# One layer of a hybrid encoder in fast matrix products: the first block's x turned token tile by token tile, its squares split anew, and four other places reordered

## The chip, the cores and the metric

The kernel runs on one core of a Trainium2 chip. The metric is the device time of one execution in microseconds, taken over several runs; lower is better. A core has five engines that run side by side, each working through its own instructions in order: TensorE (PE in the profile; PEld is its loading of weights), VectorE (DVE), ScalarE (ACT), GpSimd (POOL) and SyncE (SP), which here only issues DMAs. Matrix products leave TensorE in eight PSUM banks; everything else works in SBUF, and DMAs move data between SBUF and DRAM.

## The reference

For one sequence of 1024 tokens of width 2048, in float32:

```python
h = rms_norm(x, norm_w)
proj = h @ w_in                       # 2048 -> 6656 columns
rq, rk, rv, rg, aq, ak, av, ag = jnp.split(proj, splits, axis=-1)
y_ret = retention_branch(rq, rk, rv, decay_fwd, decay_bwd, gn_w, gn_b) * silu(rg)
y_att = window_attention_branch(aq, ak, av, sink) * silu(ag)
x = x + concat([y_ret, y_att]) @ w_out
return rms_norm(x, final_norm_w)
```

The retention branch has 8 heads of 128. It rotates q and k, and runs a forward and a backward scan in chunks of 128 tokens, each head with its own decay for each direction: the decay is exp(log_sigmoid(d) x distance). The two scans are added and normalised per head. The attention branch has 8 query heads on 2 key and value heads, sees 128 tokens to either side, and has a learned sink logit per head.

## The kernel before

**Arithmetic.** Each float32 operand is split in two fp32r parts: ACT casts the high part (line 87), DVE subtracts it from the source for the low part (line 84, `low`). One product of 128x128 by 128x512 is then three matmuls (lines 98 to 100, `mm3`). The projections use a scheme of fast products: a block of 512 columns by one half of the 2048 features is computed with seven products, numbered `PRODUCTS = (1, 2, 6, 5, 7, 3, 4)`, instead of eight, at the price of sums and differences of quarters of both operands.

**The order of the work.** There are 26 units of work, (feature half, block of columns), in four phases: `EARLY` blocks on half 0; `EARLY` and `LATE` on half 1; `LATE` and `GATES` on half 0; `GATES` on half 1. After them come four units of the output projection (`OUT`), each of seven products. `advance()` is called after every six matmuls of the projections; it raises `clock[0]` and lets every job that is under way take one step. So jobs (turning the second half of x, keeping and reloading combined operands, attention, retention, gating) are generators, whose `yield` hands back to the matmuls until the next such tick, and `idle(n)` waits n ticks.

The order of instructions on PE, SP and POOL is that in which the code is written (`manual_schedule`, line 113). ACT and DVE are ordered by the framework's planner instead, from its own timing; only within `all_manual` (line 415, closed at line 293, at the end of the first block) do all five keep the written order.

**The weights' operands.** `prepare()` (line 265) takes the next weight operand, made by `operand` or `wide`: one cast `wH` on ACT and one subtraction `wL` on DVE. Two are kept (`AHEAD = 2`), and one is made while the one before it is used.

**The first block** (`first_block`, line 269) is computed without the fast scheme, in 8 steps of 4 ticks, while x is still being prepared. Tiles 0 to 7 of x are 128 tokens each; only features 0 to 1023 are needed here. Before the first matmul, `squares(t)` (line 342) sums the squares of a tile's two halves, the first on ACT and the second on DVE (both on ACT for tiles 4 and 5); a small addition on DVE and a power on POOL make 1/rms; `scale_x(t)` (line 356) multiplies the tile on DVE. `turn_x` (line 367) transposes one block of 128 features for the four tiles of one token half, and ACT evicts it, scaled by the norm's weight, which was itself turned from `vec` (lines 414 to 422). `rest_of_x` (line 846) does the other feature blocks and the second token half between ticks: turns of block k at ticks 1 to 4, squares and scalings of tiles 4 to 7 behind them, the turns of the second token half from tick 12, the sums for the fast scheme, and `put(i)`, which makes the combined operand of product i, at the ticks written in line 871. `second_part` (line 390) and `keep` (line 370) are started behind the puts.

**Retention** (`retention`, line 601) begins by loading the decays and computing their logarithms by a series of 9 terms, in small operations on 128x16 values (lines 616 to 636), then waits until the reloads (`to_load`) are through and runs its 8 heads, one after the other. **Gating** (`gating`, line 1035) loads pairs of a mixed tile and its gate, one pair every two ticks (line 1072); ACT computes SiLU and DVE multiplies (`mix_in`), six pairs behind the loads.

**The output projection** (lines 1178 to 1218) evicts each finished bank by adding it to a tile that holds the residual (`out_evict`). In the last two units `summed` (line 1123) squares the sum on ACT, and either weights it with the final norm's weight and adds up the partial sums of squares (`part`), or, if it completes a row, calls `finish` (line 1142): 1/rms on DVE and POOL, two multiplications on DVE, one on ACT, and the row's store.

Of the kernel before, what the change touches and what calls it, by code (L numbers as in the profile page):

```python
# [53 lines left out]
AHEAD = 2  # L54


@with_exitstack
def hybrid_layer_kernel(
# [210 lines left out]
    def first_block(b, of):  # L269
# [23 lines left out]
        all_manual.close()  # L293
# [48 lines left out]
    def squares(t):  # L342
        ss = st.tile([P, 2], F32, name="ss", bufs=4)
        c = [slice(i * PART, (i + 1) * PART) for i in range(2)]
        junk = [wp.tile([P, S], BF16, name="junk", tag="ct", bufs=8) for i in range(2)]
        for i in range(2):
            if i == 0 or t in (4, 5):
                nc.scalar.activation(out=junk[i], in_=xt[t][:, c[i]], func=AF.Square, accum_out=ss[:, i:i + 1])
            else:
                nc.vector.tensor_tensor_reduce(out=junk[i], in0=xt[t][:, c[i]], in1=xt[t][:, c[i]], scale=1.0, scalar=0.0,  # L350
                                               op0=ALU.mult, op1=ALU.add, accum_out=ss[:, i:i + 1])
        rs = rms[:, t:t + 1]
        nc.vector.tensor_scalar(out=rs, in0=ss[:, 0:1], scalar1=ss[:, 1:2], scalar2=D * NORM_EPS, op0=ALU.add, op1=ALU.add)
        nc.gpsimd.tensor_tensor(out=rs, in0=rs, in1=neg_half[:, 0:1], op=ALU.pow)
# [35 lines left out]
    def second_part():  # L390
# [19 lines left out]
        for sums, _ in parts[1]:  # L410
# [5 lines left out]
    all_manual.enter_context(tc.manual_schedule(engines={mybir.EngineType.PE, mybir.EngineType.SP, mybir.EngineType.Pool,  # L416
                                                         mybir.EngineType.Activation, mybir.EngineType.DVE}))
    for t in range(NT):
        load_x(t)
        if t == 0:  # L420
            for r0, n, src in ((0, KT, norm_w), (KT, RH, gn_w), (KT + RH, RH, gn_b)):
                nc.sync.dma_start(out=vec[r0:r0 + n, :], in_=src[0].rearrange("(k p) -> k p", p=P))
# [178 lines left out]
    def retention():  # L601
        with right("ret") as ret:
# [12 lines left out]
            nc.sync.dma_start(out=db, in_=dist_b)  # L615
            nc.vector.tensor_scalar(out=au, in0=dec, scalar1=-1.0, scalar2=None, op0=ALU.mult)
# [7 lines left out]
            for n in (17, 15, 13, 11, 9, 7, 5, 3, 1):  # L624
                nc.vector.tensor_tensor(out=lg, in0=lg, in1=aq, op=ALU.mult)
# [3 lines left out]
            nc.vector.scalar_tensor_tensor(out=lg, in0=lg, scalar=-2.0, in1=dec, op0=ALU.mult, op1=ALU.add)  # L629

# [203 lines left out]
    def advance():  # L834
        clock[0] += 1
        tick()
# [9 lines left out]
    def rest_of_x():  # L846
# [32 lines left out]
    squares(0)  # L879
    for t in range(4):  # L880
        if t < 3:
            squares(t + 1)
        scale_x(t)
        if t == 1:
            pv = ax()
            nc.tensor.transpose(pv[:, 0:KT + 2 * RH], vec, ident[0:KT + 2 * RH, 0:KT + 2 * RH])
            nc.scalar.copy(out=vec_t, in_=pv[:, 0:KT + 2 * RH])
            nc.vector.tensor_scalar(out=nw, in0=nw, scalar1=D ** 0.5, scalar2=None, op0=ALU.mult)
    for s, i in enumerate((1, 2)):
        hold(i, 0)  # L890
        quarters[s + 1, 0] = comb[i][:, 0], comb[i][:, 1]
# [384 lines left out]
```

## Time and profile before

| | us |
|---|---|
| median of 3 runs | 1558.56 |
| lowest, highest | 1552.38, 1559.41 |
| the profiled execution | 1555.15 |
| its span in the profile | 1552.6 |

The page of the profile gives, for each engine, its busy time and share of the span, then the chain of work that ended last, then the groups of like instructions. TensorE's busy time is nearly the whole span, so the question at each place is why it is not busy: the lines of the timeline give the start and the length of an instruction, and in brackets the idle time of its engine just before it and what ended that. The granted clock (`PEclk`) tells when TensorE ran at less than full speed. The ends of matmuls in the records are modelled; their starts are the better measure.

### The profile page before, as it was taken

The page shows a single profiled execution, that of the slowest core. Times are in us where ns is not written, and L with a number is a line of the kernel's source. Part 1 is how long each engine was busy: PE and PEld are TensorE (multiplying, and loading weights), DVE is VectorE, ACT ScalarE, POOL GpSimd, SP SyncE. Part 2 cuts the span into 40 slices and gives each one's busy share as a digit, 9 for nine tenths or more (in the row PEclk, how much of TensorE's full clock was granted, in tenths as well). Part 3 has the DMA queues.
Part 4 walks back from the last instruction along what each step waited for, and adds up shares of the span by engine and source line. Part 5 has one row for each costly group of instructions (what it writes and reads, how often), then busy time and mean ns, then how long its engine had stood idle before and what let it go on. Part 6 is the DMA issues. An engine that isn't in the chain of part 4 may idle for free.

```text
span 1552.6 us, 20710 instructions
## 1 busy us (share of the span) xinstructions
PE 1514.6 (98%) x7377; PEld 1273.9 (82%) x7377; DVE 1086.5 (70%) x2037; ACT 690.9 (44%) x1162; POOL 159.5 (10%) x166
## 2 busy tenths in 40 slices
PE   5999999999999999999999999999999999999996
PEld 4788888788888888878888888888878888888885
DVE  5765585456857585757977797779755966775866
ACT  6643353224535363534344434543444553532425
POOL 1000001111110000001212100001211102020001
PEclk9999999999999999999999999999999999999999
DMA  7277645899764325677777566479698689395746
GB/s 284 84 258 249 225 170 160 234 239 230 185 203 136 122 83 177 228 277 203 150 190 196 162 196 204 155 268 311 164 283 204 141 242 201 83 215 169 212 161 244
DMA packets 160326, 306.60 MB, mean 197 GB/s; under 512 B 15040, under 2 KB 80992, under 8 KB 151776
## 3 DMA queue, kind: packets, MB, share of 16 engines
q1 hardware_dynamic: 140640, 269.63, 51.2%
q0 software_dynamic: 19584, 35.66, 15.2%
q8 instruction: 58, 0.95, 0.3%
q14 instruction: 44, 0.36, 0.1%
HBM read 190.68 MB, written 122.95 MB: 202 GB/s over the span
## 4 chain that ended last, share of the span: by engine, by line
PE 88%; DVE 4%; DMA 4%; ACT 2%; issue 1%; SPq 1%; POOL 0%; POOLq 0%; DVEq 0%; ACTq 0%
PE pj L100 23%; PE pj L98 23%; PE pj L99 23%; PE ax L99 4%; PE ax L100 4%; PE ax L98 4%; PE ax L727 2%; PE ax L462 1%; DMA g<-pr 1%; DVE wL L84 1%; PE ax L540 1%; PE ax L364 1%; DMA yt<-pr 1%; PE ax L774 1%; PE ax L694 1%
## 5 line engine op out<-in xcount | busy, mean ns | idle before, releaser
L98 PE MATMUL pj<-c,wH 128*128 128x512 f32 x1448 | 582.2, 402 | 1.4 <-ACT wH L87 1.4
L100 PE MATMUL pj<-c,wL 128*128 128x512 f32 x1448 | 569.4, 393 | 5.3 <-DVE wL L84 5.3
L99 PE MATMUL pj<-c,wH 128*128 128x512 f32 x1448 | 567.7, 392 | 0.0
L84 DVE TENSOR_TENSOR wL<-a,wH 128x1024 fp32r<-128x1024 f32 x184 | 225.0, 1223 | 173.8 <-ACT wH L87 172.6
L100 PEld LDWEIGHTS pj<-c,wL 128*128 128x128 f32 x1448 | 273.5, 189 | 67.0 <-DVE wL L84 8.5
L98 PEld LDWEIGHTS pj<-c,wH 128*128 128x128 f32 x1448 | 274.0, 189 | 51.3 <-ACT wH L87 1.8
L99 PEld LDWEIGHTS pj<-c,wH 128*128 128x128 f32 x1448 | 274.1, 189 | 49.5
L87 ACT CAST wH<-a 128x1024 fp32r<-128x1024 f32 x184 | 193.4, 1051 | 264.8 <-PE pj L99 117.4
L253 ACT COPY ct<-pj 128x512 f32<-128x512 f32 x200 | 115.9, 584 | 195.3 <-PE pj L100 194.5
L243 POOL DMA_DIRECT2D pr<-ct x104 | 92.2, 961 | 844.3 <-DVE ct L91 733.7
L91 DVE TENSOR_TENSOR ct<-pj,ct 128x512 f32<-128x512 f32 x170 | 114.4, 689 | 80.5 <-PE pj L100 76.5
L99 PE MATMUL ax<-wL,c 128*128 128x512 f32 x224 | 87.4, 390 | 1.8 <-DVE wL L84 1.8
L99 PE MATMUL pj<-wL,c 128*128 128x512 f32 x224 | 87.5, 391 | 0.1
L98 PE MATMUL ax<-wH,c 128*128 128x512 f32 x224 | 87.3, 390 | 0.2 <-DVE r L91 0.2
L100 PE MATMUL ax<-wH,c 128*128 128x512 f32 x224 | 87.3, 390 | 0.0
L100 PE MATMUL pj<-wH,c 128*128 128x512 f32 x224 | 87.3, 390 | 0.0
L98 PE MATMUL pj<-wH,c 128*128 128x512 f32 x224 | 87.3, 390 | 0.0
L87 ACT CAST sH<-st 128x128 fp32r<-128x128 f32 x112 | 31.1, 298 | 51.8 <-DVE st L741 37.7
L84 DVE TENSOR_TENSOR wL<-s,wH 128x1024 fp32r<-128x1024 f32 x31 | 37.7, 1216 | 19.7 <-ACT wH L87 19.7
L99 PEld LDWEIGHTS ax<-wL,c 128*128 128x128 f32 x224 | 42.1, 188 | 10.8 <-DVE wL L84 2.2
L99 PEld LDWEIGHTS pj<-wL,c 128*128 128x128 f32 x224 | 42.1, 188 | 9.5 <-DVE wL L84 0.9
L98 PEld LDWEIGHTS ax<-wH,c 128*128 128x128 f32 x224 | 42.1, 188 | 9.2 <-issue 0.5
(194 smaller groups left out, 2015.4 us busy)
## 6 DMA issues: line engine op xcount, KB each, us to landing
a<-in_w_in_dram SPq DMA_DIRECT2D x104, 512.0 KB, 4.6
kept<-c SPq DMA_DIRECT2D x28, 1024.0 KB, 7.0
c<-kept SPq DMA_DIRECT2D x28, 1024.0 KB, 9.2
pr<-ct SPq DMA_DIRECT2D x104, 256.0 KB, 5.2
pr<-ct POOLq DMA_DIRECT2D x104, 256.0 KB, 6.2
rx<-pr SPq DMA_DIRECT2D x148, 64.0 KB, 4.4
a<-in_w_out_dram SPq DMA_DIRECT2D x18, 512.0 KB, 5.2
xt<-in_x_dram SPq DMA_DIRECT2D x16, 512.0 KB, 8.7
```

What stands on the lines that cost most here:

```text
L84: nc.vector.tensor_tensor(out=dst, in0=src, in1=high.bitcast(F32), op=ALU.subtract)
L87: nc.scalar.copy(out=dst_h, in_=src)
L91: nc.vector.tensor_tensor(out=dst, in0=a, in1=b, op=ALU.add)
L98: nc.tensor.matmul(po, aH, bH, start=first, stop=False, **kw)
L99: nc.tensor.matmul(po, aH, bL, start=False, stop=False, **kw)
L100: nc.tensor.matmul(po, aL, bH, start=False, stop=last, **kw)
L243: nc.gpsimd.dma_start(out=dst, in_=t, accum_op=ALU.add)
L253: nc.scalar.copy(out=t, in_=bank)
L364: nc.tensor.transpose(pt[:, blk(i)], part, ident)
L462: nc.tensor.transpose(pt[:, blk(t)], src[:, blk(b * 4 + t)], ident)
L540: nc.tensor.transpose(pt[:, blk(j)], s[:, blk(j)], ident)
L727: nc.tensor.matmul(p, k_tok[:, c], vd[:, c, d], start=True, stop=True)
```

## The change

The change touches five places.

*First block.* The three loads of `vec` are issued from ACT's queue, ahead of all x loads, instead of from SP's behind the first tile. The transposes of the first token half run token tile by token tile, into four banks (`pts`), each tile's four right behind its scaling, instead of all four tiles for one feature block at a time. Behind tile 1's transposes stand 6, and behind tile 2's 10, transposes of the unit matrix into a bank that nothing reads. `squares` takes one half of a tile at a time, and which engine; of the eight halves of tiles 4 to 7, ACT squares three instead of six, DVE five instead of two, and three of DVE's now stand between the turns of the first four ticks. The second token half is turned from tick 11 instead of 12, and the puts of products 6, 5, 7 and 4 stand at ticks 22, 26, 32 and 37 instead of 23, 25, 33 and 36. The region in which all engines keep the written order ends at tick 33 instead of at the end of the block.

*Decays.* Four ticks pass between the loads of the decays and the first operation on them, and the series is cut in pieces, with a tick ahead of the terms 17, 11 and 5 and one ahead of the exponentials.

*Gating.* A pair is loaded every three ticks instead of two.

*Last rows.* From product 4 of the last unit on, all engines keep the written order. Weightings are put off by three, the finishing of rows by five steps (a step is the three matmuls of one `mm3`). The addition for a row's 1/rms moves from DVE to POOL.

*Last operand.* The weight operand for the second half of the last product is prepared ahead of the last eviction of the product before it.

```diff
+ORDERED = {getattr(mybir.EngineType, n) for n in ("PE", "SP", "Pool", "Activation", "DVE")}
...
-        all_manual.close()
...
-    def squares(t):
...
-            if i == 0 or t in (4, 5):
...
+    def squares(t, i, act):
...
+        if act:
+            nc.scalar.activation(out=junk, in_=c, func=AF.Square, accum_out=ss[:, i:i + 1])
+        else:
+            nc.vector.tensor_tensor_reduce(out=junk, in0=c, in1=c, scale=1.0, scalar=0.0,
+                                           op0=ALU.mult, op1=ALU.add, accum_out=ss[:, i:i + 1])
+        if i == 1:
...
+    for r0, n, of in ((0, KT, norm_w), (KT, RH, gn_w), (KT + RH, RH, gn_b)):
+        nc.scalar.dma_start(out=vec[r0:r0 + n, :], in_=of[0].rearrange("(k p) -> k p", p=P))
     for t in range(NT):
         load_x(t)
-        if t == 0:
-            for r0, n, src in ((0, KT, norm_w), (KT, RH, gn_w), (KT + RH, RH, gn_b)):
-                nc.sync.dma_start(out=vec[r0:r0 + n, :], in_=src[0].rearrange("(k p) -> k p", p=P))
...
             nc.sync.dma_start(out=db, in_=dist_b)
+            yield from idle(4)
...
             for n in (17, 15, 13, 11, 9, 7, 5, 3, 1):
+                if n % 6 == 5:
+                    yield
...
             nc.vector.scalar_tensor_tensor(out=lg, in0=lg, scalar=-2.0, in1=dec, op0=ALU.mult, op1=ALU.add)
+            yield
...
     def advance():
         clock[0] += 1
+        if clock[0] == 33:
+            all_manual.close()
         tick()
...
             turn_and_split(1, k, 0, comb[2])
-        squares(4)
+            if k != 2:
+                squares(*{0: (4, 0), 1: (4, 1), 3: (5, 0)}[k], False)
+        for t in (6, 7):
+            yield
+            if t == 6:
+                squares(5, 1, True)
+            squares(t, 0, True)
+            squares(t, 1, False)
+            scale_x(t - 2)
         yield
-        for t in range(4, NT):
-            if t + 1 < NT:
-                squares(t + 1)
-            scale_x(t)
-            yield
-        yield from idle(12 - clock[0])
+        scale_x(6)
+        scale_x(7)
+        yield from idle(11 - clock[0])
...
-            yield from idle({6: 23, 5: 25, 7: 33, 4: 36}[i] - clock[0])
+            yield from idle({6: 22, 5: 26, 7: 32, 4: 37}[i] - clock[0])
...
+    pts = [ax() for k in range(M)]
+    idling = pj()
...
+    for t in range(5):
+        if t < 4:
+            squares(t, 0, True)
+            squares(t, 1, False)
+        if t > 0:
+            scale_x(t - 1)
+            if t == 4:
+                prepare()
+            for k in range(M):
+                nc.tensor.transpose(pts[k][:, blk(t - 1)], xt[t - 1][:, blk(k)], ident)
+            for _ in range({2: 6, 3: 10}.get(t, 0)):
+                nc.tensor.transpose(idling[:, 0:P], ident, ident)
     for k in range(M):
-        turn_and_split(0, k, 0, comb[1])
+        nc.scalar.activation(out=src0[:, 0, k, half(0)], in_=pts[k], func=AF.Copy, scale=nw[:, k:k + 1])
+        split(comb[1][:, 0, k], comb[1][:, 1, k], src0[:, 0, k, half(0)])
...
-                        yield from idle(2)
+                        yield from idle(3)
...
+    def after(steps, what, *args):
+        later.append((at_now[0] + steps, what, args))
+
+    def due(every=False):
+        while later and (every or later[0][0] <= at_now[0]):
+            _, what, args = later.popleft()
+            what(*args)
...
+        if whole:
+            rs = op.tile([P, 1], F32, name="rs", bufs=4)
+            nc.gpsimd.tensor_scalar(out=rs, in0=ssq[:, tt, 3:4], scalar1=part[tt], scalar2=1.0 / D, op0=ALU.add, op1=ALU.mult)
+            nc.gpsimd.tensor_tensor(out=rs, in0=rs, in1=neg_half[:, 0:1], op=ALU.pow)
+            after(5, finish, rs, r, rt[u, 3 - n, m, t], tt, g)
+        elif u == 3:
+            after(3, weighted, r, tt, g, True)
+        else:
+            weighted(r, tt, g, False)
+            stores.append((True, res[tt][:, half(g)], r))
...
+            if (u, i) == (3, 4):
+                wo_.enter_context(tc.manual_schedule(engines=ORDERED))
...
                 if k == M - 1:
+                    if (u, i, t) == (3, 5, M - 1):
+                        prepare()
                     out_evict(u, i, t, bank[t], held)
+                at_now[0] += 1
+                due()
...
+    due(True)
     wo_.close()
```

More of the change, by code (lines that the diff above doesn't have):

```diff
@@ L340, in load_x @@
             nc.sync.dma_start(out=xt[t][:, c], in_=x[blk(t), c])
-    def squares(t):
[L343 to L346, printed above, removed]
-            if i == 0 or t in (4, 5):
[L348 to L354, printed above, removed]
+    sums_of = {}
+    def squares(t, i, act):
+        if t not in sums_of:
+            sums_of[t] = st.tile([P, 2], F32, name="ss", bufs=4)
+        ss, c = sums_of[t], xt[t][:, i * PART:(i + 1) * PART]
+        junk = wp.tile([P, S], BF16, name="junk", tag="ct", bufs=8)
+        if act:
[4 more added lines that the diff above has]
+        if i == 1:
+            rs = rms[:, t:t + 1]
+            nc.vector.tensor_scalar(out=rs, in0=ss[:, 0:1], scalar1=ss[:, 1:2], scalar2=D * NORM_EPS, op0=ALU.add, op1=ALU.add)
+            nc.gpsimd.tensor_tensor(out=rs, in0=rs, in1=neg_half[:, 0:1], op=ALU.pow)
     def scale_x(t):
@@ L877, in rest_of_x @@
         start(keep(0))
[L879 to L891, printed above, removed]
-    prepare()
+    pv = pj()
+    nc.tensor.transpose(pv[:, 0:KT + 2 * RH], vec, ident[0:KT + 2 * RH, 0:KT + 2 * RH])
+    nc.scalar.copy(out=vec_t, in_=pv[:, 0:KT + 2 * RH])
+    nc.vector.tensor_scalar(out=nw, in0=nw, scalar1=D ** 0.5, scalar2=None, op0=ALU.mult)
+    pts = [ax() for k in range(M)]
+    idling = pj()
+    for i, t in enumerate((1, 2)):
+        hold(t, 0)
+        quarters[i + 1, 0] = comb[t][:, 0], comb[t][:, 1]
+    for t in range(5):
[10 more added lines that the diff above has]
+                nc.tensor.transpose(idling[:, 0:P], ident, ident)
     for k in range(M):
-        turn_and_split(0, k, 0, comb[1])
+        nc.scalar.activation(out=src0[:, 0, k, half(0)], in_=pts[k], func=AF.Copy, scale=nw[:, k:k + 1])
+        split(comb[1][:, 0, k], comb[1][:, 1, k], src0[:, 0, k, half(0)])
     start(rest_of_x())
@@ L1121, in prefill @@
             nc.sync.dma_start(out=e, in_=res[4 * (m - 1) + t][:, half(2 * OUT[u][1] + n - 1)])
+    at_now, later = [0], deque()
+    def after(steps, what, *args):
[4 more added lines that the diff above has]
+            what(*args)
     def summed(u, n, m, t):
         r, tt, g = rt[u, n, m, t], 4 * (m - 1) + t, 2 * OUT[u][1] + n - 1
-        op, fw, ssq = (pools[n] for n in ("op", "fw", "ssq"))
+        op, ssq = pools["op"], pools["ssq"]
         whole = u == 3 and (n, m) in ((2, 1), (1, 2))
@@ L1136, in summed, with finish @@
             nc.vector.tensor_scalar(out=part[tt], in0=part[tt], scalar1=D * NORM_EPS, scalar2=None, op0=ALU.add)
-        if u == 2:
-            stores.append((True, res[tt][:, half(g)], r))
-        if whole:
-            finish(r, rt[u, 3 - n, m, t], tt, g)
-    def finish(r, r1, tt, g):
-        op, fw, ssq = (pools[n] for n in ("op", "fw", "ssq"))
-        rs = op.tile([P, 1], F32, name="rs", bufs=4)
-        nc.vector.tensor_scalar(out=rs, in0=ssq[:, tt, 3:4], scalar1=part[tt], scalar2=1.0 / D, op0=ALU.add, op1=ALU.mult)
-        nc.gpsimd.tensor_tensor(out=rs, in0=rs, in1=neg_half[:, 0:1], op=ALU.pow)
+    def finish(rs, r, r1, tt, g):
         g1 = 4 * OUT[3][1] + 1 - g
-        row = rows_a[tt]
+        fw, row = pools["fw"], rows_a[tt]
         nc.vector.scalar_tensor_tensor(out=row[:, half(g)], in0=r, scalar=rs, in1=fw[:, half(g)], op0=ALU.mult, op1=ALU.mult)
```

11 lines of the change are left out of this document (6 added, 5 removed).

## The prediction

> **What bounds the kernel.** The page first: TensorE (PE) is busy nearly all the time and carries the chain that ended last, so the end moves only by time in which PE waits or runs at a lower clock.
>
> ```profile
> span 1552.6 us, 20710 instructions
> PE 1514.6 (98%) x7377; PEld 1273.9 (82%) x7377; DVE 1086.5 (70%) x2037; ACT 690.9 (44%) x1162; POOL 159.5 (10%) x166
> PE 88%; DVE 4%; DMA 4%; ACT 2%; issue 1%; SPq 1%; POOL 0%; POOLq 0%; DVEq 0%; ACTq 0%
> ```
>
> 1552.6 - 1514.6 = 38 us is all that waiting is worth, and 16.9 of it lies in the first 20 us, 11.5 after 1540 (rows below). Then the largest of PE's waits past the start (us in all, times, longest), and busy time by stretches (columns: length, PE, PEld, DVE, ACT, POOL busy, granted clock, DMA share, GB/s).
>
> ```profile
> PE pj L100 <- DVE wL L84: 5.3, 6, 1.8
> 0.00:20.00 20.00, 3.12 (x11) 2.15 (x12) 9.81 (x19) 7.88 (x13) 4.22 (x10) 1.00 0.90 326
> 40.00:60.00 20.00, 18.30 (x88) 14.44 (x87) 8.63 (x14) 12.21 (x20) 1.06 (x2) 0.91 0.24 79
> 680.00:700.00 20.00, 18.22 (x74) 14.61 (x73) 8.82 (x35) 6.35 (x14) 0.00 (x0) 0.91 0.93 314
> 1160.00:1180.00 20.00, 19.65 (x80) 16.09 (x80) 10.22 (x14) 8.28 (x14) 1.75 (x2) 0.91 0.79 200
> 1540.00:1553.00 13.00, 1.48 (x7) 0.90 (x5) 4.56 (x10) 4.39 (x7) 1.10 (x2) 0.75 0.74 306
> ```
>
> Three stretches show a granted clock of 0.91. A loss of 0.09 x 20 = 1.8 us follows each of three stalls, so a stall that goes can take its clock dip along. Elsewhere PE is full, and the edits have nothing to win there.
>
> **The first block.** The code counts ticks: one per six matmuls, 6 x 0.227 = 1.36 us at the full clock (0.23 between the starts at 70.49 and 70.72, below). The timeline of PE, DVE and ACT (start, length, engine, line; in brackets the idle time before and what ended it):
>
> ```profile
> 17.38 0.47 PE L364 MATMUL ax<-ident,xt 128*128 128x128 f32 x1 [2.09 <-DVE xt L358]
> 18.58 3.03 PE L364 MATMUL ax<-ident,xt 128*128 128x128 f32 x13 [0.72 <-DVE xt L358]
> 19.09 0.69 ACT L365 ACTIVATE src<-ax,vec_t 128x512 f32<-128x512 f32 x1 [1.43 <-PE ax L364]
> 21.84 0.63 PE L99 MATMUL pj<-c,wH 128*128 128x512 f32 x1
> 22.26 0.63 PE L100 MATMUL pj<-c,wL 128*128 128x512 f32 x1
> 42.24 0.75 DVE L358 TENSOR_SCALAR xt<-xt,rms 128x1024 f32<-128x1024 f32 x1 [0.44 <-POOL rms L354]
> 43.04 0.33 PE L364 MATMUL ax<-ident,xt 128*128 128x128 f32 x1 [0.86 <-DVE xt L358]
> 44.18 0.50 PE L100 MATMUL pj<-c,wL 128*128 128x512 f32 x1 [0.35 <-DVE wL L84]
> ```
>
> Before, the last x tile releases 13 transposes at once (3.03 / 13 = 0.233 us each); turned tile by tile it leaves 4. But the unit-matrix transposes stand in the same queue: tile 2's four and the ten behind them issue from 17.38, and at 0.233 us end at 20.64. Tile 3, ready at 18.58, starts 2.06 us late, and ACT's first eviction moves from 19.09 to about 21.1: no matter that PE has nine transposes fewer behind it, ACT now sets the pace.
>
> Moving the three vec loads from SP to ACT's queue frees SP, whose second x tile is issued at 2.83 behind them:
>
> ```profile
> 1.64 0.43 SPq L422 DMA_DIRECT2D vec<-in_norm_w_dram  x1
> 2.83 4.15 SPq L340 DMA_DIRECT2D xt<-in_x_dram  x6
> ```
>
> That is worth 0 (the vec loads still pass the DMA engines) to 1.2 us (2.83 - 1.64); I take the middle, 0.6, since no row separates issue from transfer. On ACT's queue they are issued before x lands, when ACT has nothing else; the copy of vec_t, now ahead of the first square, may hold that one, which has 2.6 us of slack per tile behind the loads.
>
> So is the clock slow while PE only transposes? The 13 transposes fill 3.03 us, yet the matmuls behind them still start 0.42 us apart (21.84, 22.26) instead of 0.227. (The granted clock reads 1.00 there; its record seems to begin with the first change, so I go by the starts.) I take: transposes do not raise it.
>
> The Trainium skill, "TensorE: Matmul & The Clock Gate", Part 4, says the full clock does not engage for transposes; by that the added ones are a pure cost. This trace agrees as far as it goes.
>
> What decides is not the first matmul but scale_x(7), on which the second token half waits (42.24, PE released 43.04). Before, ACT squares six halves of tiles 4 to 7, in a row from 31.43, and DVE's last two squares follow:
>
> ```profile
> L348 ACT ACTIVATE junk<-xt 128x1024 bf16<-128x1024 f32 x6 | 6.3, 1045 | 0.0
> L350 DVE CUSTOM_DVE_ANT_0 junk<-xt 128x1024 bf16<-128x1024 f32 x2 | 2.4, 1218 | 0.0
> L84 DVE TENSOR_TENSOR c<-src,c 128x512 fp32r<-128x512 f32 x8 | 5.5, 692 | 5.6 <-ACT c L87 5.6
> L84 DVE TENSOR_TENSOR wL<-a,wH 128x1024 fp32r<-128x1024 f32 x3 | 3.7, 1224 | 1.0 <-ACT wH L87 1.0
> ```
>
> The new split gives ACT 3 and DVE 5. ACT, paced by four evictions and casts of 0.69 + 0.62 less 0.07, reaches the second wH at 19.09 + 4 x 1.24 = 24.05; DVE starts its wL at 25.1, shifted by +2.0 - 0.6 = 26.5. From there DVE has 2 wL, 4 lows, 5 squares, 4 small sums and 4 scalings: 2 x 1.22 + 4 x 0.69 + 5 x 1.30 + 4 x 0.21 + 4 x 0.75 = 15.5 us, less 0.08 by which each of 19 overlaps the one before: 14.0. With 0.5 of waiting for casts and for POOL's power, scale_x(7) ends near 41.0, against 42.24 + 0.75 = 42.99.
>
> PE now asks at tick 11 instead of 12. It has twelve ticks and one turn done at 41.0 + 0.1 + 1.36 = 42.46, against 43.14: 0.7. The wL behind the scaling is then at 42.2, no longer late (0.35), and PE's wait here falls from 0.86 and 0.49 (its third transposition and its fourth) to about 0.6 in one piece, so that no dip follows (1.8, the 0.91 of the stretch from 40). Together 2.8. Ends: 1.2 (no help from vec, a slow clock for longer) and 4.2 (the added transposes delay nothing).
>
> The hand-kept order now reaches to tick 33 instead of 32. Before, the subtractions of put(7) ran ahead of a wL:
>
> ```profile
> 65.06 1.22 DVE L94 TENSOR_TENSOR src<-src 128x1024 f32<-128x1024 f32 x1
> 70.49 0.39 PE L98 MATMUL pj<-c,wH 128*128 128x512 f32 x1
> 70.72 0.39 PE L99 MATMUL pj<-c,wH 128*128 128x512 f32 x1
> 72.01 0.50 PE L100 MATMUL pj<-c,wL 128*128 128x512 f32 x1 [0.91 <-DVE wL L84]
> ```
>
> They are written at tick 33, yet the first ran at 65.06, tick 24: past the hand-kept region ACT and DVE are placed by a planner wherever it believes them ready. With put(7) at tick 32 and kept in order they no longer stand there, and 1.29 - 0.23 = 1.07 us go. That the puts move by a tick costs nothing: their products come 16 or more ticks later. second_part's loads and keep's stores move a tick on SP with them; PE waited for none of these before. Block: **-3.9**.
>
> **Decays in steps.** The stall:
>
> ```profile
> 690.98 0.17 DVE L616 TENSOR_SCALAR passing<-passing 128x16 f32<-128x16 f32 x1 [5.74 <-DMA passing<-in_decay_bwd_dram]
> 694.95 1.22 DVE L84 TENSOR_TENSOR wL<-a,wH 128x1024 fp32r<-128x1024 f32 x1
> 696.23 0.50 PE L100 MATMUL pj<-c,wL 128*128 128x512 f32 x1 [1.78 <-DVE wL L84]
> ```
>
> 1.78 us idle and a dip of 1.8. DVE waits 5.74 us for a landing, then does 19 small steps (3.97 / 0.21) ahead of the wL. The loads keep their place on SP, so the landing stays where it is; idle(4) and the yields change only where the steps are written, and all of them still stand ahead of the next operand. The planner went by readiness and not by writing at 65.06. I take **0**; ends 0 and -3.6. Retention itself starts later: by 8 ticks, of which the old one spent 5 waiting for the last reload, so by 3 (4.1 us), for every head, and with it gating.
>
> **Gating in threes.** ACT waits for a gate's load while an operand stands behind it:
>
> ```profile
> 1156.50 0.63 ACT L1052 ACTIVATE yt<-yt 128x512 f32<-128x512 f32 x1 [4.73 <-DMA yt<-pr]
> 1159.09 0.50 PE L98 MATMUL pj<-c,wH 128*128 128x512 f32 x1 [1.41 <-ACT wH L87]
> 1160.35 0.50 PE L100 MATMUL pj<-c,wL 128*128 128x512 f32 x1 [0.53 <-DVE wL L84]
> 1201.16 0.50 PE L100 MATMUL pj<-c,wL 128*128 128x512 f32 x1 [0.83 <-DVE wL L84]
> 1140.00:1160.00 20.00, 18.41 (x81) 14.61 (x79) 12.40 (x14) 8.67 (x12) 5.31 (x6) 1.00 1.07 333
> ysrc<-mix SPq DMA_DIRECT2D x9, 256.0 KB, 8.7
> ```
>
> Price: 1.41 + 0.53 + 0.83, 0.4 for pipelines refilled, and a dip of 1.8 (stretch from 1160): 5.0. The DMA share is 1.07: saturated. A pair of loads (0.5 MB) every 3 ticks instead of 2 falls from 190 to 128 GB/s, a fifth of the 333. Landings (8.7 us in the middle) should shorten, and ACT's waits with them. On SP, fewer loads stand ahead of the next weights. Sixteen pairs take 48 ticks, 65 us, from about 1140 to 1205, in time for the puts, which wait for products freed from 1204 on. I take **-3.8** of 5.0, leaving one wait of about 1; ends +2 (the waits fall on other operands) and -5.0.
>
> **Rows finished late.**
>
> ```profile
> 1533.21 0.51 PE L99 MATMUL ax<-wL,c 128*128 128x512 f32 x1 [1.77 <-DVE wL L84]
> 1541.09 0.39 PE L100 MATMUL ax<-wH,c 128*128 128x512 f32 x1
> 1544.03 0.69 DVE L91 TENSOR_TENSOR r<-ax,r 128x512 f32<-128x512 f32 x1
> ```
>
> The last wL runs behind weightings and reductions of the rows. Prepared ahead of the eviction, and these put off by three steps, it is at most 0.3 late: 1.5 go, and 0.2 at the product's first matmul. After the last matmul (1541.09 + 0.39) DVE takes the bank only at 1544.03, 2.5 us late, held by rows 1 and 2. Taken at once, row 3 is stored 2 us sooner, but now row 2 leaves just ahead of it, and a row of 1 MB needs 2.5 us at about 400 GB/s: 0.7 remain. POOL's new addition lies between 0.2 us (DVE's small steps) and 1.0 and hides behind row 2's store. **-2.4**; ends -1 and -4.
>
> **Sum** against the profiled execution (1555.15 us, 2.55 of it outside the span): -3.9 - 0 - 3.8 - 2.4 = -10.1, 1545.05. The median of the runs shown lies 3.4 above that execution: 1558.56 - 10.1 = 1548.5.
>
> **Rivals.**
> - *Decays help* (0.20): the planner follows the writing after all, and the wL slips in between the steps. For: they are now written in four pieces. Against: 65.06. 3.6 more: 1544.9.
> - *The added transposes raise the clock* (0.10): tile 3 starts at once; 1.5 us more, 1547.0. Against: the starts at 21.84 and 22.26.
> - *Gating's wait only moves* (0.22): loads still land later than the planner believes, and ACT stands before another operand: 3.8 less and a dip: 1554.1.
> - *The dips are not the stalls' doing* (0.05): they stay where the stalls go, 2 x 1.8 less, 1552.1. For: the 1.77 us at 1533 had none (granted clock 1.00 there). Against: three dips, each right behind a stall.
>
>   The same page of the Trainium skill, section "Why this matters for your kernels", names gaps over about 3 us as what lowers the clock, and these are under 1.8; the measurement decides, and it shows dips behind such gaps.
> - *Retention slips* (0.11), the slower one: shifted by 3 ticks, DVE's work of a head meets other operands; one late wL per head with a dip, 0.7 (between the 0.53 and 0.83 of gating) + 1.8 = 2.5 us, times 8 = 20: 1568.5. From 1.3 us a head it eats the gain, from 2.3 it is slower beyond measuring error. Against: DVE has 9 us to spare in a head, and PE none lost:
>
> ```profile
> 770.60:821.30 50.70, 50.70 (x277) 43.52 (x276) 41.68 (x109) 22.87 (x41) 10.60 (x10) 1.00 0.69 166
> ```
>
> The forecast keeps 0.32. Half a per cent, 7.8 us, is about what a measurement of this kernel can tell from no change. Faster beyond it: 0.25 of the forecast, 0.19, 0.09, 0.04 of gating and 0.01 of the dips, 0.58; slower: 0.07 of retention's; within: 0.35. The range goes from nearly all upper ends together (-3.6 for decays, -5 and -4 at gating and the end), 1540, to a gating that only moves with a first block at its lower end, 1558.
>
> **What would show it.** Right: PE idle under 0.7 us in one piece from 40 to 75; L616 still waiting over 4 us, PE near 694 too; a DMA share under 1 in gating's first 20 us; the last row's addition within 0.2 us of the last matmul. Wrong: first matmuls 0.23 apart; no stall near 694; PE idle inside 720 to 1130.

## The result and the profile after

| | before | after |
|---|---|---|
| median, us | 1556.16 (8 runs) | 1563.62 (8 runs) |
| lowest, highest | 1552.38, 1559.41 | 1559.79, 1565.85 |
| the profiled execution, its span | 1555.15, 1552.6 | 1565.85, 1564.0 |

The changed kernel takes 1.0048 times as long, 95% interval 1.0031 to 1.0064: 7.5 us slower, where 10.1 us of gain were forecast. The page of the changed kernel, its first lines and its chain:

```profile
span 1564.0 us, 20754 instructions
...
PE 1521.1 (97%) x7393; PEld 1276.4 (82%) x7393; DVE 1088.4 (70%) x2035; ACT 687.0 (44%) x1156; POOL 161.7 (10%) x174
...
PE 84%; DMA 7%; DVE 4%; ACT 2%; issue 1%; SPq 1%; POOL 0%; DVEq 0%; POOLq 0%; ACTq 0%
```

PE still bounds the kernel, but the chain now runs through DMA for 7% instead of 4%, and PE is idle for 42.9 us instead of 38 (span less busy time; the other 6.5 us of the longer span are longer busy time). Where the time went is seen best by counting: both kernels issue the same 6384 matmuls of `mm3` in the same order, so the start of the n-th in one trace can be set against the start of the n-th in the other. The table gives that difference to the kernel before in us (negative: ahead), for the changed kernel and three of the runs told of below. A single trace scatters: e2 (below), whose five engines have the kernel before's order up to gating, is 2.8 us behind it at n = 4700, and seven other runs that share the changed kernel's order up to there lie from -4.5 to -1.8 (the changed kernel itself: -3.1). So a difference of under 3 us between two columns proves nothing by itself.

| n | before, us | after | e1 twos | e12 twos, order kept in part 1 | e13 twos, nine ticks |
|---|---|---|---|---|---|
| 0 | 21.26 | -0.55 | -0.29 | +0.38 | +0.29 |
| 95 | 52.06 | -3.58 | -3.34 | -2.66 | -2.76 |
| 287 | 100.77 | -5.46 | -5.22 | -4.54 | -4.63 |
| 1200 | 314.67 | -4.00 | -3.50 | -3.54 | -3.74 |
| 3000 | 708.39 | -5.46 | -4.89 | -4.95 | -5.02 |
| 4400 | 1074.90 | -3.76 | -4.12 | -3.91 | +8.41 |
| 4700 | 1151.17 | -3.14 | -3.41 | -3.30 | +8.90 |
| 5000 | 1224.44 | +2.02 | -2.10 | -6.81 | +11.36 |
| 5300 | 1293.10 | +1.47 | -2.73 | -5.22 | +11.55 |
| 5600 | 1361.10 | +13.05 | -2.73 | -5.22 | +12.51 |
| 6300 | 1519.76 | +13.05 | -2.73 | -5.22 | +12.51 |
| 6383 | 1541.09 | +11.48 | -4.30 | -6.78 | +10.98 |

The first block gains 5.5 us, more than forecast; 1.5 of it is given back between 270 and 290 us, 1.4 come near 695 and 1.7 go again up to 728 us; the heads of retention are passed without loss from there to 1075 us; then gating loses 16.2 us, 5.2 of them from 1151 to 1224 and 11.6 from 1293 to 1361; the end gains 1.6. So one term, gating, is wrong by 20 us, and it turns the result around. The timeline of PE in the changed kernel at those two places, with ACT's:

```profile
1199.69 0.79 PE L99 MATMUL pj<-c,wH 128*128 128x512 f32 x1 [3.11 <-ACT wH L88]
...
1302.46 0.50 PE L99 MATMUL ax<-wH,c 128*128 128x512 f32 x1 [1.36 <-ACT wH L88]
1303.72 0.50 PE L100 MATMUL ax<-wL,c 128*128 128x512 f32 x1 [0.76 <-DVE wL L85]
1324.79 0.51 PE L99 MATMUL pj<-wH,c 128*128 128x512 f32 x1 [2.94 <-ACT wH L88]
```

```profile
1197.10 0.63 ACT L1074 ACTIVATE g<-g 128x512 f32<-128x512 f32 x1 [3.89 <-DMA g<-pr]
...
1198.58 1.06 ACT L88 CAST wH<-a 128x1024 fp32r<-128x1024 f32 x1
...
1300.85 0.63 ACT L1074 ACTIVATE g<-g 128x512 f32<-128x512 f32 x1 [3.85 <-DMA g<-pr]
1301.38 1.03 ACT L88 CAST wH<-a 128x1024 fp32r<-128x1024 f32 x1
...
1310.13 0.63 ACT L1074 ACTIVATE g<-g 128x512 f32<-128x512 f32 x1 [2.62 <-DMA g<-pr]
...
1321.22 0.63 ACT L1074 ACTIVATE g<-g 128x512 f32<-128x512 f32 x1 [9.26 <-DMA g<-pr]
1321.76 2.03 ACT L1209 COPY ct<-ax 128x512 f32<-128x512 f32 x4
1323.66 2.02 ACT L88 CAST wH<-a 128x1024 fp32r<-128x1024 f32 x2
```

Read each time from PE back: it waits for a cast `wH`; the cast stands on ACT behind a SiLU; the SiLU waits for its gate to land. The busy time by stretches (columns as in the prediction; the seventh number is the granted clock) shows what the stalls draw after them:

```profile
1190.00:1210.00 20.00, 16.85 (x62) 12.87 (x61) 14.41 (x16) 9.83 (x14) 2.85 (x4) 0.83 0.58 140
...
1290.00:1310.00 20.00, 17.88 (x70) 14.02 (x69) 9.03 (x13) 5.33 (x7) 4.49 (x7) 0.91 0.93 238
1310.00:1335.00 25.00, 21.19 (x80) 16.56 (x79) 14.16 (x13) 8.46 (x14) 5.37 (x7) 0.86 0.69 125
```

0.17 x 20, 0.09 x 20 and 0.14 x 25 are 3.4, 1.8 and 3.5 us lost to the clock alone. SP's timeline of the changed kernel tells why the last gates come so late (L983 loads a weight of the output projection, L1091 a mixed tile, L1092 its gate):

```profile
1303.69 0.38 SPq L983 DMA_DIRECT2D a<-in_w_out_dram  x1
1304.13 0.46 SPq L1091 DMA_DIRECT2D ysrc<-mix  x1
1304.68 0.38 SPq L1092 DMA_DIRECT2D g<-pr  x1
1310.85 0.38 SPq L983 DMA_DIRECT2D s<-in_w_out_dram  x1
1311.29 0.53 SPq L1091 DMA_DIRECT2D ysrc<-mix  x1
1311.91 0.49 SPq L1092 DMA_DIRECT2D g<-pr  x1
```

One pair goes out behind each weight load, and a weight load waits for the tile that an operand's subtraction (`wL`) frees: 49.6 us in eight waits from 1230 to 1330. The gate issued at 1304.68 has its SiLU at 1310.13, ahead of the next pair's load at 1311.29: the SiLU stands not six pairs behind its load, as the code is written, but right behind it. For the last one (1321.22 - 9.26 = 1311.96) ACT turned to it as soon as its gate's load was issued (1311.91), and waits 9 us for the landing. In the kernel before, gating's loads end earlier (its last SiLU starts at 1289.7 us, here at 1321.2), so there is less of the output projection for them to disturb.

### The profile page after: what moved, and what is told of

The parts are those of the page before. It is cut to its first block, busy times and chain, and to the rows that moved or that the text cites. A ratio compares the mean times of both kernels' runs of the same rounds, so it can differ in the third digit from the quotient of the medians.

```text
span 1564.0 us, 20754 instructions
## 1 busy us (share of the span) xinstructions
PE 1521.1 (97%) x7393; PEld 1276.4 (82%) x7393; DVE 1088.4 (70%) x2035; ACT 687.0 (44%) x1156; POOL 161.7 (10%) x174
## 4 chain that ended last, share of the span: by engine, by line
PE 84%; DMA 7%; DVE 4%; ACT 2%; issue 1%; SPq 1%; POOL 0%; DVEq 0%; POOLq 0%; ACTq 0%
PE pj L101 22%; PE pj L99 22%; PE pj L100 21%; PE ax L101 4%; PE ax L100 4%; PE ax L99 4%; DMA g<-pr 2%; PE ax L733 2%; DVE wL L85 1%; PE ax L464 1%; DMA yt<-pr 1%; PE ax L542 1%; PE ax L780 1%; DMA xt<-in_x_dram 1%; PE ax L700 1%
## 5 line engine op out<-in xcount | busy, mean ns | idle before, releaser
L244 POOL DMA_DIRECT2D pr<-ct x104 | 92.1, 960 | 849.3 <-DVE ct L92 734.4
L99 PEld LDWEIGHTS pj<-wH,c 128*128 128x128 f32 x224 | 42.7, 191 | 12.3 <-ACT wH L88 3.4
```

The costliest lines, as they stand in the source:

```text
L99: nc.tensor.matmul(po, aH, bH, start=first, stop=False, **kw)
L244: nc.gpsimd.dma_start(out=dst, in_=t, accum_op=ALU.add)
```

## The experiments

"Kept order" below means the written order on all five engines, as in the first block, instead of the planner's on ACT and DVE. "Twos" and "threes" are the ticks from pair to pair in gating.

**e1 and e2: the spacing alone, taken out and put in.**

```diff
 # e1: the changed kernel; e2: the kernel before, with 3 for 2
                         todo.append((d, g))
-                        yield from idle(3)
+                        yield from idle(2)
```

> The changed kernel with gating's pairs loaded every two ticks again; all else stays changed. Theory S (the spacing): by threes the loads run on to 1312 us, among the weight loads of the output projection, and ACT stands before a gate that has not landed with an operand's cast behind it; after's stalls past 1190 (3.3 and 2.6 and 4.3 us, with clock dips of 6.8, 3.4 and 6.8 us at half speed) cost about 18.6 us against 2.7 of before there. S expects 1563.6 - 15.9 = about 1548, and PE without a stall over 1.5 us from 1190 to 1400. Rival L (lateness): retention's three ticks push gating into the output projection, the spacing matters little: 1558 or more, with stalls near 1300 still there.

> The kernel before with the one edit that gating's pairs are loaded every three ticks. S expects the loss of the changed kernel to appear here: 1556.2 + 12 to 16 = 1568 to 1572, with PE stalls of 2 us and more between 1190 and 1330 and dips behind them. L expects less than 4 us: 1560 or less, since gating starts as early as before.

Measured: e1 1550.09 us, 0.9962 of the kernel before (0.9947 to 0.9977); e2 1570.26 us, 1.0085 (1.0068 to 1.0101). Both fall where S expects them. The spacing costs about 14 us in either kernel, and lateness of three ticks has no part in it: e2 starts gating at the same tick as the kernel before. The instructions of the SiLU's line and what ACT waited for ahead of them (us, times), in the kernel before and the changed kernel (the first column of the first line: shortest, middle and longest duration in ns, then the first and last start):

```profile
L1052 ACT ACTIVATE g<-g x16: 625/632/647, 1158.9 to 1289.7; 128x512 f32<-128x512 f32 x16
...
  DMA yt<-pr: 24.6, 13
  DMA g<-pr: 19.2, 11
```

```profile
L1074 ACT ACTIVATE g<-g x16: 627/632/645, 1155.6 to 1321.2; 128x512 f32<-128x512 f32 x16
...
  DMA g<-pr: 36.8, 12
  DMA yt<-pr: 31.2, 13
```

As many waits, but 68.0 us instead of 43.8: 2.7 us each instead of 1.8 (in e1 44.9). With twos two pairs go out behind one weight, and the second lands while ACT waits for the first (in e1 near 1176 us the waits are 3.92 and then 0.68 us); with threes often one pair goes out behind a weight, and each waits for itself. That is read from the timelines; no run tests it apart.

**e3: the decays in one piece again**, with twos: `idle(4)` and the three `yield`s taken out.

> The changed kernel with gating by twos and the decays in one piece again (no wait behind their loads, no pieces). Theory D0 (the prediction's reading: the edit of the decays is worth nothing, since the planner goes by readiness): within 1.5 us of the run with gating by twos alone, the stall near 690 as long (about 2 us), and the small stalls at 714, 723 and 1076 of the changed kernel (0.83, 0.64, 0.46 us) gone if they come from the retention that starts three ticks later. Rival D1 (the pieces let the weight operand in): the stall near 690 grows by over 1 us or regains its clock dip, 2 to 4 us slower.

Measured: 1550.24 us against 1550.09. D0 holds in the time, and the stall near 690 is as long (2.05 us against 2.09, both by the starts of matmuls). Of the small stalls, the one at 714 is gone in e1 already, and those at 723 and 1076 are there in e3 too, a little shifted (0.44 and 0.46 us), so they don't come from the three ticks. One sign of D1 did come in e3's trace: behind the stall near 690 the dip is back (granted clock 0.91 from 680 to 700, 1.00 in e1), and e3 is 2.0 us behind e1 over that place. It isn't the pieces' doing: e5 has them, and the changed kernel's order on every engine up to gating, and has the dip too (last section).

**e4: no transposes of the unit matrix**, with twos: the loop of 6 and 10 taken out.

> The changed kernel with gating by twos and without the sixteen transposes of the unit matrix. Theory W (the added transposes raise the clock): the granted clock is no longer full before the first matmul, the first matmuls start 0.42 us apart again for some 3 us, 1.5 us lost, and tile 3's transposes come up to 2 us sooner: within 2 us of the run with gating by twos alone, first matmuls 0.42 apart. Rival C (a pure cost, the clock rises by the other transposes or by none): first matmul 2 us sooner and the whole 2 us faster, with the spacing of the first matmuls unchanged.

Measured: 1548.96 us, 0.9954 (0.9940 to 0.9969). The timeline of PE in the changed kernel, whose first block e1 shares, and in e4:

```profile
17.88 1.30 PE L913 MATMUL pj<-ident 128*128 128x128 f32 x10
19.01 0.60 PE L911 MATMUL ax<-ident,xt 128*128 128x128 f32 x4
20.71 0.50 PE L99 MATMUL pj<-c,wH 128*128 128x512 f32 x1 [1.10 <-ACT c L88]
...
22.00 0.39 PE L99 MATMUL pj<-c,wH 128*128 128x512 f32 x1
22.23 0.40 PE L100 MATMUL pj<-c,wH 128*128 128x512 f32 x1
```

```profile
16.85 2.31 PE L911 MATMUL ax<-ident,xt 128*128 128x128 f32 x8 [1.48 <-DVE xt L362]
19.95 0.79 PE L99 MATMUL pj<-c,wH 128*128 128x512 f32 x1 [0.79 <-ACT c L88]
...
21.69 0.63 PE L99 MATMUL pj<-c,wH 128*128 128x512 f32 x1
22.12 0.63 PE L100 MATMUL pj<-c,wH 128*128 128x512 f32 x1
```

W holds: without them the first matmul comes 0.8 us sooner than in the changed kernel, but the matmuls start 0.43 us apart instead of 0.23, and by matmul 11 e4 is 0.8 us behind e1 (from the first matmul on it loses 1.0 us on the kernel before, e1 gains 0.8). At matmul 95 both are equally far (-3.27 and -3.34): the second token half, which waits for `scale_x`, takes the gain back. So the added transposes raise the clock, and this is worth nothing to the kernel. That e4 ends 1.1 us ahead of e1 is within the spread of their four runs each (1.5 and 1.3 us); its trace lacks the stalls that e1 has near 276 and 288.

**e5: gating's loads on POOL's queue**, with threes: `nc.gpsimd.dma_start` for both loads.

> The changed kernel, pairs still every three ticks, but their loads (mixed tile and gate) issued from POOL's queue instead of SP's. Theory Q (the queue): on SP a pair stands behind a weight load that waits until an operand is made, so it is issued several us after it is written, while the planner has placed its SiLU by the written time; off SP the loads go out at their ticks, and the PE stalls past 1190 us (3.3, 2.6, 4.3) go: 1550, plus or minus 3. Rival P (the placing alone): the planner puts the SiLU ahead of the landing whatever the queue, and the stalls stay: 1558 to 1566.

Measured: 1570.34 us, 1.0107 (1.0088 to 1.0125); ACT waits 71.8 us ahead of its SiLUs. This lies outside the ranges of both Q and P, and decides nothing on Q, because the queue wasn't free. POOL's timeline in e5 (L244 is an accumulating store):

```profile
1178.22 0.54 POOL L1092 DMA_DIRECT2D g<-pr  x1
1188.50 1.82 POOL L244 DMA_DIRECT2D pr<-ct  x2 [9.74 <-DVE ct L92]
1189.69 1.22 POOL L1091 DMA_DIRECT2D ysrc<-mix  x1
```

A pair stands behind a store that waits for an eviction, as on SP behind a weight that waits for a tile. A queue that really waits for nothing wasn't tried.

**e6 and e7: kept order through gating**, with threes and twos.

```diff
+        kept_order = ExitStack()
+        kept_order.enter_context(tc.manual_schedule(engines=ORDERED))
         yield from gating()
+        kept_order.close()
```

> The changed kernel, pairs every three ticks from SP, but all engines keep the written order while gating runs, so that a SiLU stands on ACT where it is written, six pairs (18 ticks, 25 us) behind its loads. Theories Q and P both blame that ACT's SiLU waits for a landing with an operand's cast behind it, and expect ACT to wait no more than 1 us for a gate and the stalls past 1190 to go: 1546 to 1551. Rival T (it is the traffic: loads among the out-projection's weight loads make the weights land late, whatever ACT does): stalls of the same size stay, 1558 to 1566, the casts then waiting for the weights' DMA.

> As the kept order of the run before, with pairs every two ticks. If ACT's waits for gates are all that is left of gating's loss, the stalls at 1148 to 1158 (0.97, 0.69, 1.25, 0.69) and 1198 (0.72) with their dip go: 4 to 6 us below the run with twos alone, 1544 to 1546. If twos land too late for a written distance of 12 ticks (16 us), stalls stay, within 2 us of 1550.

Measured: 1566.02 us, 1.0076 (1.0060 to 1.0093), and 1565.64 us, 1.0078 (1.0057 to 1.0100): e6 lies at the upper edge of rival T's range and e7 in no range; by the totals Q and P are missed. By place they tell more. Through the first part's loads (n 4700 to 4900) both gain 5.2 us on the kernel before, where the changed kernel loses 3.4; ACT's waits ahead of SiLUs fall from 68.0 to 6.1 us in e6:

```profile
L1077 ACT ACTIVATE g<-g x16: 613/628/652, 1171.9 to 1325.4; 128x512 f32<-128x512 f32 x16
...
  DMA g<-pr: 6.1, 3
```

Rival T falls here: in the second part, among the output projection's weights, e6 loses 0.2 us (n = 5100 to 5500) where the changed kernel loses 11.0, with the same loads at the same spacing. What is lost comes behind each part: from n = 4900 to 5000 e6 loses 14.5 us and e7 11.5. The kept order holds there for the combined operands as well. ACT's timeline in e7:

```profile
1213.09 1.05 ACT L88 CAST c<-yt 128x1024 fp32r<-128x1024 f32 x1 [3.69 <-DVE yt L95]
1217.82 1.04 ACT L88 CAST c<-yt 128x1024 fp32r<-128x1024 f32 x1 [3.69 <-DVE yt L95]
...
1221.35 1.04 ACT L88 CAST wH<-a 128x1024 fp32r<-128x1024 f32 x1 [1.51 <-DVE a L95]
```

Twice ACT waits 3.69 us for a subtraction of a `put`, with the next `wH` behind it: the same fault with DVE as the one waited for. PE stands 4.8 us there.

**e8: two edits far apart**, with twos: kept order from the loads of the decays to their exponentials and nine ticks instead of four; and in the last unit the residual's half is weighted together with 1/rms in one operation of `finish`, instead of in `weighted`.

> Pairs by twos, and two edits far apart, read from the trace at their own places. (1) Decays: the written order is kept from their loads to the exponentials, and nine ticks pass instead of four. If the pieces failed only because the planner goes by readiness, DVE's first operation of the decays waits under 0.5 us, the stall near 690 (2.1 us) goes, and the stream gains 2 us there; if the landing is what is late in any case, it stays. (2) Last rows: the residual's half is no longer weighted in an operation of its own; the multiplication by 1/rms weights it in one. If the three weightings ahead of row 1's addition are what starts the stores late (stores begin 1.1 us before the last matmul, before the change 2.3 us), the span's end comes 1.0 to 1.6 us sooner behind the last matmul (from 11.5 us to about 10); if the stores are bound by the last row, it stays at 11.5.

Measured: 1562.19 us, 1.0047 (1.0032 to 1.0063). The decays in the timeline of DVE, first the changed kernel, then e8:

```profile
687.12 0.17 DVE L619 TENSOR_SCALAR passing<-passing 128x16 f32<-128x16 f32 x1 [5.91 <-DMA passing<-in_decay_bwd_dram]
```

```profile
686.95 0.17 DVE L621 TENSOR_SCALAR passing<-passing 128x16 f32<-128x16 f32 x1 [0.22 <-DMA passing<-in_decay_bwd_dram]
```

The wait is gone and with it PE's wait for `wL` near 690: with nine ticks the pieces do what they are written for once the order is kept (with four ticks and the order kept no run was made). But PE then waits 1.11 us for a reloaded operand and 1.78 for a `wL` at 713, and from n = 3000 to 4600 the stream falls from 6.3 ahead to 7.0 behind, in stalls of 0.5 to 1.2 us in the heads. At the end the span closes 10.6 us behind the last matmul's start instead of 11.5: 0.9 of the 1.0 to 1.6 expected. The last `wL` is then 1.0 us late again, so nothing is won in sum.

**e9, e10 and e12: kept order only while pairs are loaded**, from a part's first load to its last SiLU; e9 with twos, e10 with threes, e12 with twos in the first part alone.

```diff
+                    if (s, m) == (0, 0):
+                        kept_order.enter_context(tc.manual_schedule(engines=ORDERED))
                     for i in range(s * M, (s + 1) * M):
...
                 while todo:
                     mix_in()
                     yield
+                kept_order.close()
```

> The changed kernel, pairs every two ticks, the written order kept only from a part's first load to its last SiLU, and not through the combined operands that follow. If the kept order of the run before helped through the loads (it gained 5.2 us on the kernel before from 1151 to 1200, the run with twos alone lost 1.3 there) and lost only because the casts of the combined operands then stood ahead of the weights' (stalls of 1.8, 5.0 and 1.4 us from 1196 to 1237), this keeps the gain and drops the loss: 1550 - 6.6 = 1543.5, up to 1548 if the one late gate of the second part (8.4 us of waiting at 1303, stall 1.5 and 1.0 and a dip) stays. If the loss comes with the kept order itself, 1552 or more.

> The same with pairs every three ticks. If the spacing costs only through SiLUs that the planner puts ahead of their landings, it is harmless here: 1543 to 1548, within 3 us of the run with twos, and no PE stall over 1.5 us from 1190 to 1330. If the traffic among the out-projection's weights costs by itself (rival T), 1552 or more, with stalls from 1240 to 1330.

> The changed kernel, pairs every two ticks, the written order kept only while the first part's pairs are loaded; the second part is the planner's again. From the runs before, by matmuls of the same number against the kernel before: with the order kept the stream is 7.1 us ahead behind the first part, and the planner's second part loses 0.6; then 1.6 at the last operand. Theory P (what costs is a SiLU put ahead of its landing with a cast behind it, and each part is as before): 1556 - 9.3 = about 1546, 3 to 4 us below both the run with twos alone and the one with the order kept in both parts. Rival: the parts are not independent, the second loses again as the planner starts it from another state: 1549 or more.

Measured: e9 1549.21 us, 0.9962 (0.9950 to 0.9974); e10 1553.28 us, 0.9984 (0.9975 to 0.9994); e12 1549.40 us, 0.9964 (0.9952 to 0.9976). With threes the kept order takes back 10.3 of the 13.5 us that the spacing costs (1563.62 to 1553.28, against 1550.09): most of the loss is the place of the SiLUs. The other 3 to 4 us stay with the spacing: e10 has stalls of 1.9 and 1.7 us at 1204 and 1206, where the `wH` waits 4.23 us for an addition on DVE that stands behind a put's subtractions, two of gating's multiplications and two evictions in the written order, and of 1.8 and 1.0 at 1313. So the expected 1548 was missed, and by its two signs (1552 or more, stalls from 1240 to 1330) e10 would be rival T's. But what the cast at 1314.18 stands behind is not a weight's landing:

```profile
1313.64 0.63 ACT L1074 ACTIVATE g<-g 128x512 f32<-128x512 f32 x1 [4.67 <-DMA g<-pr]
```

It is once more a gate's. SP issued that load only at 1305.76, after waiting 10.5 us for the multiplication that frees a gate's tile: the kept order holds the tile longer, and with it the load. In twos the kept order is 4.7 us ahead of e1 behind the first part (n = 5000, e12), and then gives it back: in e9, which misses its 1543.5 to 1548, a last gate is 9.1 us late with an operand behind it; in e12 the planner's second part loses 1.6 where it lost 0.6 in e1. By its time e12 is its rival's (1549 or more); that the parts are not independent is not shown, since 1 us between two traces is within their scatter. e1, e3, e4, e9 and e12 beat both kernels, by 6 to 7 us on the kernel before, and can't be told apart.

**e11: the small steps off DVE**, with twos: the decays' series (in one piece) and the negation of the sink on POOL.

> The changed kernel with pairs every two ticks, the decays in one piece again, and the operations that wait for the small landings taken off DVE: the series of the decays and the negation of the sink run on POOL. Theory D (a wait for a landing costs only where a weight operand is queued behind it): the stalls at 690 (2.1 us) and 275.8 (1.65 us) go, 1546 to 1547. Rival O (POOL's own queue pays): POOL waits 5 to 6 us for the landing and takes 10 to 20 us for the series, the accumulating stores behind it come late, evictions run out of tiles, and PE stalls near 700 by 2 us or more: 1550 or more. The series takes other but equal steps.

Measured: 1554.10 us, 0.9991 (0.9979 to 1.0003). Neither theory in full: the wait doesn't go and POOL's queue isn't what pays. DVE's and ACT's timelines in e11:

```profile
695.27 0.29 DVE L686 TENSOR_SCALAR dT<-df,lg 128x128 f32<-128x128 f32 x1 [8.31 <-POOL lg L634]
```

```profile
695.27 0.30 ACT L636 ACTIVATE qd<-lg,stp 128x8 f32<-128x8 f32 x1 [9.08 <-POOL lg L634]
...
696.92 1.98 ACT L88 CAST wH<-a 128x1024 fp32r<-128x1024 f32 x2
```

The wait moved along the chain to the next reader, on two engines at once, and there a `wH` stands behind it: PE stalls 2.5 and 1.1 us near 695 instead of 2.1 near 690. The sink's stall at 275.8 is gone, but a new one of 1.7 us stands at 286, where DVE waits 8.5 us for a tile to be rotated.

**e13: nine ticks and no kept order**, with twos.

> The changed kernel with pairs by twos and nine ticks instead of four behind the loads of the decays, no order kept. In the run with nine ticks and the order kept, the stream lost 10 us from 710 to 1130 against the run with twos alone. If that is the later retention (the prediction's slower rival, retention slips), it comes here too: 1558 to 1561, PE stalls of 0.4 to 1.2 us on the transposes of y and the state's matmuls in most heads. If it is the kept order around the decays, this run is within 2 us of 1550, with no such stalls.

Measured: 1565.29 us, 1.0057 (1.0036 to 1.0077). The nine ticks alone do it: the first head starts at matmul 3102 instead of 3054, eight ticks later than before, and 13.4 us go from n = 3000 to 4400. Of these 5.7 are one stall of 4.0 us at 714 (a `wL`) with its dip of 1.7; the rest, and 0.5 behind it, are small stalls as in e8, about 1 us a head. Three ticks cost nothing in the heads (the changed kernel keeps -3.8 from 728 to 1075 us), eight cost 13 us or more in all.

## Why the prediction was wrong

**Gating in threes** (forecast -3.8, ends +2 and -5; measured +16.2 from n = 4700 to 5600, and +14 by e1 and e2). The step that failed is "Landings (8.7 us in the middle) should shorten, and ACT's waits with them". The landings hardly did, and the waits grew. The DMA share of gating's first 20 us is 1.08 (1.07 before), where a value under 1 was to be seen, and the row of 8.7 us (mixed tiles issued from 1133 to 1160, from issue to landing) is now 7.9:

```profile
1140.00:1160.00 20.00, 18.22 (x76) 14.36 (x75) 13.44 (x17) 9.58 (x16) 3.97 (x5) 0.95 1.08 307
ysrc<-mix SPq DMA_DIRECT2D x8, 256.0 KB, 7.9
```

Over both parts the mixed tiles took 7.0 us in the middle against 6.1 before, the gates 7.0 against 6.2 (tiles `g`) and 5.6 against 6.3 (`yt`). ACT's waits rose from 43.8 to 68.0 us. The step says nothing of where the SiLUs stand, and holds only if they stand behind their loads as written. Yet the same prediction had found at 65.06 us that the planner puts ACT and DVE by readiness and not by writing. Used here, that says: a SiLU stands right behind its load, so each pair is a wait, however far apart the pairs are; e6 and e10 show that this place is what costs. The step's own row at 1156.50, a SiLU that waits 4.73 us for its landing, says it too: at a distance of six pairs, 16 us, there would be little to wait for. "In time for the puts" counts the first part's sixteen pairs alone; the second part, which loads among the output projection's weights up to 1312 us and lost 11.6, has no term in the sum. The rival "gating's wait only moves" (0.22) had the mechanism, priced at 5.6 us above the forecast instead of 20.

**The first block** (forecast -3.9; measured -5.5 by 100 us). Right in kind: PE waits 0.33 and 0.49 us ahead of 40 us and not at all from there to 75, the dip is gone, and put(7) brought 1.2 for the 1.07 forecast (n = 143 to 191). "I take: transposes do not raise it" was wrong (e4), and cost the forecast little: tile 3 was held up 0.9 us instead of 2.06, the ten transposes taking 0.13 us each instead of 0.233, so ACT's first eviction came at 19.32 instead of 21.1. The rival on that clock (0.10) held in kind. Its price, 1.5 us, is about what the block gained beyond the forecast (1.6), but it isn't the clock's gain: e4, without these transposes, is as far ahead at matmul 95. `scale_x(7)` ended at 39.8 us instead of 41.0. The loss of 1.5 us near 280 wasn't foreseen. DVE waits 4.5 us for the sink's landing ahead of a `wL` in both kernels (stalls of 0.96 and before 1.06 us); new is a stall of 1.1 us at 288, behind a wait of 7.1 us for a tile to be rotated (5.6 before, without a stall). That the shifted stream meets this landing elsewhere is likely, and not tested.

**Decays** (0; measured 0 by e3). The reason held as well: L619 still waits 5.9 us; nine ticks don't help without the order (6.05 us in e13) and do with it (0.22 in e8). The dip behind that stall went all the same (-1.4), which is luck: e5 has it with the same order of instructions. Then 1.7 are lost up to 728, with small stalls at 714 and 723 (0.83 and 0.64 us). The rival that the dips are not the stalls' doing (0.05) is not settled: the dip after 40 us went with its stall, this one went while its stall stayed.

**Rows finished late** (-2.4; measured -1.6). The last operand gave 1.57 of 1.7. The 0.7 behind the last matmul shrank to 0.1: the row's addition came at once, as forecast (last matmul's end 1552.57 + 0.39, addition 1553.01), but the first of the last stores now begins 1.1 us ahead of the last matmul's start, before 2.3, so the rows leave closer together. SP's lines, before and after:

```profile
1538.77 9.65 SPq L1153 DMA_DIRECT2D out_dram<-ra  x5
```

```profile
1551.50 7.15 SPq L1189 DMA_DIRECT2D out_dram<-ra  x5
```

e8, without the weightings ahead of the first row, won 0.9 us back; that weightings are the whole reason is argued, not shown.

**Retention slips** (0.11, 1568.5): not at three ticks. e13 shows that it is real at eight, 1565.29, but not as priced: instead of a late `wL` with a dip in each head, 2.5 us, there is one ahead of the first head, 5.7 us, and then about 1 us a head in small stalls, with no dip among them.

Without gating the forecast's terms sum to -6.3, and e1, which is that kernel, measured 1550.09 - 1556.03 = -5.9. Part of that is luck: -5.5 instead of -3.9 in the first block, +1.5 near 280, the dip near 695 that stayed away.

## What to carry to other kernels

Where a planner orders an engine, look up in the trace where the consumer of a load stands, not in the code: spacing loads out in the source moves the loads, and not the wait, and each consumer that is pulled up behind its load holds whatever stands behind it. A wait for a landing is harmless only on an engine that has nothing urgent queued; moving the waiting step to another engine passed the wait to the next reader here (e11). Where the written order is kept to cure it, keep it only over the stretch in which the waits lie, and see what else it freezes.

## What the runs showed of the hardware

*Transposes raise the clock.* In the changed kernel, with nothing but transposes on PE up to 20.71 us, the ten at 17.88 take 0.13 us each and tile 3's four behind them 0.15, while the thirteen before took 0.233, and the first matmuls start 0.23 apart. The trace's record of the clock begins, at full, at 17.95 us; in e4 at 24.74, in the kernel before at 24.17. The Trainium skill, "TensorE: Matmul & The Clock Gate", Part 4, says that the full clock does not engage for transposes; here the measurement differs, and decides.

*A stall of 1.7 to 1.9 us may or may not draw a dip.* The stall near 690 is 1.73 us long in the changed kernel, 1.78 before (at 694) and 1.80 in e5, which has the changed kernel's order of instructions up to there. The stretch in the changed kernel, then in e5:

```profile
680.00:700.00 20.00, 18.27 (x80) 14.52 (x80) 12.66 (x39) 5.84 (x13) 2.63 (x3) 1.00 0.95 324
```

```profile
680.00:700.00 20.00, 17.73 (x69) 13.67 (x69) 10.72 (x37) 5.02 (x13) 1.76 (x2) 0.91 0.91 317
```

The clock is 1.00 in the first, 0.91 in e5 and before; in e2, which has the order of the kernel before, the stall is 1.85 us and the clock 1.00. So length alone doesn't decide, and neither does the order of instructions; what does stays open. In the trace's record each dip up to the last matmul is half the clock for 3.41 us or, as from 1199 behind a stall of 3.11, for 6.83: 1.7 or 3.4 us lost. The same page of the Trainium skill, section "Why this matters for your kernels", names gaps over about 3 us as what lowers the clock; the dip of 1.8 us from 1290 follows waits of 1.36 and 0.76 us, so the measurement differs from this too.
